# Holding TensorE to source order in the delta-rule stage of a hybrid block

## The chip, the cores and the metric

The kernel runs on one core of one Trainium2 chip. The metric is device time in microseconds (us) of one execution. Of TensorE (PE, with its weight loads PEld), VectorE (DVE), ScalarE (ACT), GpSimd (POOL) and the DMA queues (issued by SP), each runs its own instruction stream in order and meets the others at semaphores.

## The reference

One layer on a sequence of 2048 tokens with 1024 channels, all in float32:

```python
h = rms_norm(x, mix_norm_g); proj = h @ w_in          # 3*512 + 4*512 + 8 columns
y_a = short_conv_mixer(a_h, a_b, a_c, ...)             # b * conv3(c * hx), normed per group of 64
y_b = gated_deltanet(d_q, d_k, d_v, d_z, beta, alpha)  # conv4 + silu, chunked delta rule, norm, gate
x = x + concat([y_a, y_b]) @ w_out
x = x + hier_moe(rms_norm(x), ...)                     # 4 groups x 8 experts, top 2
return rms_norm(x, final_norm_g)

# gated delta rule, per chunk and head
uw = triangular_solve(eye + L, [v * beta, k_beta * exp(g)])
v_new = u_i - w_i @ state
o_i = qd_i @ state + a_i @ v_new
state = state * exp(gl_i) + kd_i.T @ v_new
```

## The kernel before

The program has three stages. The first, up to about 941 us of the profiled span, computes the input projection together with the two mixers; the second multiplies by `w_out` and routes; the third runs the experts. The change touches only the first.

The first stage is cut into 16 **units**, one for each of 4 heads and 4 blocks of 512 tokens (`units`, head outermost). A unit goes through three steps, written as Python generators that yield between pieces:

- `stage1` does four projections (q, k, v, z) with `project`. One projection is 24 matmuls of 128x128 by 128x512 in float16 (the rows `acc<-hT,whl`, L134), because both operands are split in a high and a low half, and it yields after every fourth. ACT copies each result out, DVE runs the four-tap convolutions (`cv`, L298, L301), ACT and DVE the silu (`sg`, L305 to L310).
- `stage2` takes `cv` to the matrices of the delta rule: transposes of k (`d<-id,cv`, L326), decays (`grow,sel` L342, then ACT's exponential `eG` L345 that reads the same PSUM tile, then a mask that is added to that tile, `mneg` L346, then ACT's `DT` L349), k·k and q·k products (`d<-cv`, L363), and on DVE the solve of the 16x16 diagonal blocks (`Ts`, L389 to L391).
- `stage3` completes the inverse by doubling (L420 to L461) and runs the scan over four chunks of 128 tokens: `r<-Sn,kq` (L472), DVE's `xr`, `r<-xr,U` (L477), DVE's `vn`, `r<-vn,kd` (L483), DVE's new state `Sn`, and the outputs `o` (L491, L492). It ends with ACT's square of `o` (`osq`, L497), DVE's sum (L498), a matmul with a constant matrix (`d<-osq,omean`, L501), and ACT, DVE and POOL work (L96, L97, L503, L504) up to the output `yh`.

From the fifth unit on (`FIRST = NB`, that is 4) each unit also carries one piece of the short-convolution mixer: `conv_a`, three more projections, DVE work (L545 to L552), ACT's square (`osq`, L554), a matmul `pn<-osq,bones` (L557), ACT's L96 and L97, DVE's L559, and a split into `yh` by ACT (L92) and DVE (L93). Its `osq` and the `osq` of `stage3` are the same single buffer (pool `one`, one buffer a tag).

In the source, unit `i`'s projections are written together with `stage2` of unit `i-1` and `stage3` of unit `i-2`: `merge` takes 43 steps of `main` (one step is four projection matmuls), and between them spreads 18 steps of `stage2` and 21 of `stage3`. What is left of each is run out after the 43rd step, `main` first. But the source's order doesn't bind TensorE: a planner orders every engine's instructions when the program is built, by when it reckons their inputs to be there and by priority (steps of older units have priority 1000), so that projection matmuls of a later unit can stand ahead of a step that is written earlier. PSUM holds two projection results (`accp`), three tiles `d`, two `r` and one `o`.

Of the kernel before, what the change touches and what calls it, by code (L numbers as in the profile page):

```python
# [38 lines left out]
def hybrid_block(ctx, tc, x, mix_g, w_in, ca_w, ca_g, dn_w, a_log, dt_bias, dn_g, w_out,  # L39
                 ffn_g, rg_w, re_w, w_gate, w_up, w_down, fin_g, out, dbg=None):  # L40
    nc = tc.nc
    dbg = dbg or {}
    V, A, G, T = nc.vector, nc.scalar, nc.gpsimd, nc.tensor

    consts = ctx.enter_context(tc.tile_pool(name="consts", bufs=1))
    dram = ctx.enter_context(tc.tile_pool(name="dram", bufs=1, space=DRAM))
# [32 lines left out]
    def seq(*gs):  # L79
        for g in gs:  # L80
            yield from g
# [18 lines left out]
    with ExitStack() as ph1:  # L100
# [39 lines left out]
        def slices(g, n):  # L140
            for _ in range(n):
                if next(g, 0) == 0:
                    return
                yield 1

        def merge(main, others, steps=24):

            others = [[o[0], o[1], 0, o[2] if len(o) > 2 else 1000] for o in others]
            for i in range(steps):
                if main is not None and next(main, 0) == 0:  # L150
                    main = None
                for o in others:
                    while o[0] is not None and o[2] * steps < (i + 1) * o[1]:
                        o[2] += 1
                        with tc.high_priority(o[3]):
                            if next(o[0], 0) == 0:
                                o[0] = None
            for g in [main] + [o[0] for o in others]:
                for _ in g or ():
                    pass  # L160

        dn = ph1.enter_context(ExitStack())
        if True:
# [30 lines left out]
            def prep(b, xs=None):  # L194
                ss = two.tile([P, CB], F32, name="ss")
                for c in range(CB):
                    xt = xs[c] if xs else load_x(b, c)
                    pool, tag = (whlp, "whl") if b else (lng, "kq")
                    hh = pool.tile([P, 2, D], F16, name="hh", tag=tag)
                    A.activation(hh[:, 0], xt, AF.Square, accum_out=ss[:, c:c + 1])  # L200
                    (G if b > 1 or b and c % 2 else V).tensor_tensor(xt, xt, gmix, op=OP.mult)
                    rsqrt(ss[:, c:c + 1], ss[:, c:c + 1], 1.0 / D)
                    split(hh[:, 0], hh[:, 1], xt, ss[:, c:c + 1])
                    if b and PSPL:
                        yield 1
                    for i in range(2):
                        pt = dp.tile([P, KT, P], F16, name="d")
                        for k in range(KT):
                            pin(T.transpose(pt[:, k, :], hh[:, i, k * P:(k + 1) * P], id16), b and PPIN)
                        (A.copy if b>1 and i else V.tensor_copy)(hT[b][:, i, :, c * P:(c + 1) * P], pt)  # L210
                    yield 1
# [350 lines left out]
            def load_ws(key, cols):  # L562
                ws = wcache.setdefault(key, [])
                for c0 in cols:
                    ws.append(load_w(c0))
                    yield 1

            def cols_a(m):
                return [c0 + P * m for c0 in (1024, 0, 512)]

            FIRST = NB
# [7 lines left out]
            def main(i):  # L579
                yield from main1(i)  # L580
                if i >= FIRST:
                    yield from conv(i - FIRST)
# [108 lines left out]
            for i in range(len(units) + 2):  # L691
                others = []
                if 0 <= i - 2:
                    others.append((stage3(*units[i - 2]), S3N, S3P))
                if 0 <= i - 1 < len(units):
                    others.append((stage2(*units[i - 1]), S2N, S2P))
                if i < NB:
                    others.append((gate_cols(i) if i else gt0, GTN, GTP))
                if i + 1 < NB:
                    others.append((prep(i + 1), PREP[i], PRP))  # L700
                if i < len(units) and i % NB == NB - 1:
                    h = i // NB + 1
                    new = [load_ws(h, [1536 + 512 * q + P * h for q in range(4)])] if h < H else []
                    new.append(load_ws(H + h - 1, cols_a(h - 1)))
                    others.append((seq(*new), 7 if h < H else 3))
                if i < len(units):
                    merge(main(i), others, 43 if i >= FIRST else 24)
                else:
                    merge(slices(rest, 32), others)
            dn.close()  # L710

            o1 = ctx.enter_context(tc.tile_pool(name="o1", bufs=2, side="right", reuse_waits="tile"))
# [835 lines left out]
```

## Time and profile before

| | |
|---|---|
| median of 3 runs | 1977.12 us (1973.57 to 1978.59) |
| the profiled execution | 1979.14 us, of which the span 1977.4 us |
| busy over the span | PE 1768.5 us (89%), DVE 1414.9 (72%), ACT 1016.1 (51%), POOL 492.0 (25%) |
| 203 to 941 us, fifth unit to the last of the mixers | PE busy 711.93 of 738.00 us, DVE 506.45, ACT 267.39, POOL 107.94 |

Times below are microseconds from the start of the span. A row of the timeline gives start, duration, engine, line, operation, output and inputs, shapes, count, and in square brackets how long the engine had stood idle before it and what it had waited for. A float32 matmul is two or more PE instructions.

### The profile page before, as it was taken

Reading aid. Unit: us, or ns where it says so; the run is one execution under the profiler, and the core shown is the slowest. Engines: PE = TensorE matmul, PEld = TensorE weight load, DVE = VectorE, ACT = ScalarE, POOL = GpSimd, SP = SyncE. Lnnn points to the kernel's source line nnn. Section 1 sums busy time; section 2 is a strip of 40 time slices with the busy share of each in tenths; the row PEclk is TensorE's granted clock in tenths of the full one; section 3 lists DMA queues with packets and bytes.
Section 4 is the critical chain, followed back from the end, with each engine's and each line's share of the span. In section 5 each row is a group of like instructions: output and inputs, shape, how many; then the busy total and the mean of one; then the engine's idle time right before and its main releaser. Section 6 shows DMA issues by size and latency. Waiting matters only on the chain. (4 is left out here: it accounts for less than half of the span.)

```text
span 1977.4 us, 43048 instructions
## 1 busy us (share of the span) xinstructions
PE 1768.5 (89%) x16783; PEld 1218.5 (62%) x16783; DVE 1414.9 (72%) x2756; ACT 1016.1 (51%) x1700; POOL 492.0 (25%) x408
## 2 busy tenths in 40 slices
PE   6789999999999999999899998999899999999830
PEld 5455555555555455554354466988788999999720
DVE  8899776776678666764444858887778888888623
ACT  6655333443334333322433656766677777777622
POOL 1321111111111111101000114233222443443366
PEclk9889999999999999999999999999999999999965
DMA  4221000110002000101656868999999999999854
GB/s 152 71 73 52 10 14 14 55 47 14 14 24 77 9 14 9 35 20 41 213 172 230 303 215 267 340 295 293 297 318 358 358 343 347 340 341 300 275 164 146
DMA packets 203764, 329.26 MB, mean 167 GB/s; under 512 B 45021, under 2 KB 99366, under 8 KB 203554
## 3 DMA queue, kind: packets, MB, share of 16 engines
q1 hardware_dynamic: 177010, 264.90, 39.5%
q0 software_dynamic: 22016, 52.48, 10.2%
q10 hardware_dynamic: 4528, 9.06, 1.2%
q8 instruction: 134, 2.20, 0.4%
q14 instruction: 76, 0.62, 0.1%
HBM read 276.21 MB, written 54.53 MB: 167 GB/s over the span
## 5 line engine op out<-in xcount | busy, mean ns | idle before, releaser
L134 PE MATMUL acc<-hT,whl 128*128 128x512 f16 x2640 | 637.7, 382 | 0.5 <-DVE hT L210 0.3
L1080 PE MATMUL a<-xT,wgu 128*128 128x136 f16 (+19 forms) x6528 | 401.3, 224 | 16.5 <-DVE sl L1087 15.6
L1080 PEld LDWEIGHTS <-wgu 128*128 128x128 f16 x6528 | 395.0, 99 | 22.0 <-issue 17.6
L134 PEld LDWEIGHTS <-whl 128*128 128x128 f16 x2640 | 252.9, 99 | 250.1 <-issue 12.4
L93 DVE SCALAR_TENSOR_TENSOR wgu<-mst,gw,wgu 128x1024 f16<-128x1024 f32 x256 | 317.2, 1276 | 16.6 <-ACT wgu L92 13.9
L92 ACT ACTIVATE wgu<-mst,gw 128x1024 f16<-128x1024 f32 x256 | 279.7, 1138 | 32.0 <-DMA mst<-in_w_up_dram 30.2
L1000 PE MATMUL a<-wo,yb 128*128 128x512 f16 x768 | 177.9, 381 | 5.3 <-ACT wo L92 3.8
L1093 POOL DMA_INDIRECT acc_d<-yo,tabS x53 | 101.0, 1905 | 256.0 <-ACT yo L1141 204.9
L93 DVE SCALAR_TENSOR_TENSOR wd<-mst,wd 128x1024 f16<-128x1024 f32 x128 | 154.4, 1214 | 6.5 <-ACT wd L92 6.5
L1150 PE MATMUL a<-ac,wd 128*128 128x136 f16 (+12 forms) x1920 | 143.1, 230 | 4.4 <-ACT ac L92 4.1
L92 ACT ACTIVATE wd<-mst 128x1024 f16<-128x1024 f32 x128 | 130.8, 1046 | 27.2 <-DMA mst<-in_w_down_dram 26.3
L1150 PEld LDWEIGHTS <-wd 128*128 128x128 f16 x1920 | 130.3, 98 | 7.7 <-issue 6.0
L1000 PEld LDWEIGHTS <-yb 128*128 128x128 f16 x768 | 71.8, 98 | 86.2 <-issue 11.4
L301 DVE SCALAR_TENSOR_TENSOR cv<-raw,pcol,cv 128x512 f32<-128x512 f32 x144 | 120.1, 834 | 2.2
L1049 POOL DMA_INDIRECT xr<-h_d,tabG x54 | 69.1, 1280 | 169.4 <-PE t L1065 147.3
L1087 DVE SCALAR_TENSOR_TENSOR sl<-a,sl 128x136 f32<-128x136 f32 (+19 forms) x136 | 39.5, 292 | 78.7 <-ACT sl L1086 78.3
L1086 ACT ACTIVATE sl<-a 128x136 f32<-128x136 f32 (+19 forms) x136 | 37.1, 275 | 100.8 <-PE a L1080 98.0
L1115 PE MATMUL pl<-wd,ac 128*120 128x512 f16 (+6 forms) x336 | 80.4, 384 | 0.7 <-ACT ac L92 0.7
L1054 POOL DMA_INDIRECT gs<-gt_d,gix x54 | 76.4, 1415 | 16.3 <-issue 15.4
L1137 PE MATMUL pl<-id,yt 128*128 128x128 f32 (+13 forms) x320 | 55.3, 293 | 27.9 <-ACT yo L1141 18.5
L389 DVE TENSOR_TENSOR pr<-Ts,fs 32x1 f32<-32x1 f32 (+14 forms) x240 | 74.7, 311 | 5.2 <-DMA fs<-dscr 1.4
L92 ACT ACTIVATE ac<-sl 128x136 f16<-128x136 f32 (+19 forms) x136 | 41.9, 310 | 63.7 <-DVE sl L1087 63.6
(359 smaller groups left out, 2578.7 us busy)
## 6 DMA issues: line engine op xcount, KB each, us to landing
mst<-in_w_gate_dram SPq DMA_DIRECT2D x256, 256.0 KB
mst<-in_w_up_dram SPq DMA_DIRECT2D x256, 256.0 KB
mst<-in_w_down_dram SPq DMA_DIRECT2D x128, 512.0 KB
wst<-in_w_in_dram SPq DMA_DIRECT2D x28, 512.0 KB
xt<-in_x_dram SPq DMA_DIRECT2D x16, 512.0 KB
ydr<-yh SPq DMA_DIRECT2D x64, 128.0 KB
yb<-ydr SPq DMA_DIRECT2D x16, 512.0 KB
x<-in_x_dram SPq DMA_DIRECT2D x16, 512.0 KB
```

The costliest lines, as they stand in the source:

```text
L92: A.activation(hi, src, AF.Copy, scale=scale)
L93: (eng or V).scalar_tensor_tensor(lo, src, scale, hi, op0=OP.mult, op1=OP.subtract)
L134: T.matmul(acc, w[:, i, k, :], hT[b][:, j, k, :], start=(n == 0), stop=(n == 3 * KT - 1))
L301: V.scalar_tensor_tensor(y, tap(j), pcol[:, q:q + 1], y, op0=OP.mult, op1=OP.add)
L389: V.tensor_tensor(q, Ts[:, 0:i, 0:i].rearrange("p j m -> p m j"), bc(fs[:, None, 0:i, i], [32, i, i]), op=OP.mult)
L1000: T.matmul(po, yb[:, i, k, c * P:(c + 1) * P], wo[:, j, k, n * FF:(n + 1) * FF], start=(q == 0), stop=(q == 3 * KT - 1))
L1049: G.indirect_dma_start(out=xr[0:cw].rearrange("p a k c -> p (a k c)"), out_offset=None, in_=h2_d[0:end, :], in_offset=IO(ap=ix, axis=0))
L1054: G.indirect_dma_start(out=g[0:cw], out_offset=None, in_=gt_d[0:end * NE, :], in_offset=IO(ap=gx, axis=0))
L1080: T.matmul(pg[:, q, 0:n], wq[:, i, k, q, f * P:(f + 1) * P], xT[:, j, k, 0:n], start=(z == 0), stop=(z == 3 * KT - 1))
L1093: st = G.indirect_dma_start(out=acc_d, out_offset=IO(ap=sx, axis=0), in_=yo[0:cw], in_offset=None, bounds_check=S - 1, oob_is_err=False, c ...
L1115: T.matmul(py[0:n], ac[:, i, k, 0:n], wd[:, j, k, q * FF:(q + 1) * FF], start=(z == 0), stop=(z == 3 * FF // P - 1))
L1150: T.matmul(pg[:, u, 0:n], wd[:, i, k, d * P:(d + 1) * P], ac[:, j, k, 0:n], start=(z == 0), stop=(z == 3 * FF // P - 1))
```

## The change

All TensorE instructions now go through a small wrapper. While `pinned[0]` is set, each instruction is tied behind the TensorE instruction that was written before it. It is set from the unit with index 4 to the end of the loop over units (two more rounds, which hold only older units' steps and the remaining mixer pieces), and cleared behind it. No operation, tile or size changes, and nothing is tied on the other engines.

```diff
-    V, A, G, T = nc.vector, nc.scalar, nc.gpsimd, nc.tensor
+    V, A, G = nc.vector, nc.scalar, nc.gpsimd
+    pinned = [False]
+
+    class InOrder:
+        def __getattr__(self, name):
+            f = getattr(nc.tensor, name)
+
+            def call(*args, **kw):
+                ins = f(*args, **kw)
+                return tc.keep_in_program_order(ins) if pinned[0] else ins
+
+            return call
+
+    T = InOrder()
...
+                pinned[0] = i >= FIRST
                 if i < len(units):
                     merge(main(i), others, 43 if i >= FIRST else 24)
                 else:
                     merge(slices(rest, 32), others)
+            pinned[0] = False
             dn.close()
```

In the built program the number of TensorE instructions is the same (16,136 matmuls). Their order differs from the 1,185th to the 4,473rd; ACT, DVE, POOL and SP are reordered in the same stage alone. Every TensorE instruction now bears the wrapper's line, L53, and lines of other engines stand 15 higher.

**The seam between two units, on TensorE.** Before, where the unit with index 4 ends and the next begins (`acc_2736` is the last projection of the one, `acc_2804` the first of the other; `pn` is the mixer's norm, `r`, `o` and `d<-osq` belong to the scan of an older unit):

```order
L134 MATMUL acc_2736<-hT0_90,whl_2276 128x512
L483 MATMUL r_2782<-vn_2759,kd_1961 128x128
L491 MATMUL o_2599<-kq_1959,Sn_2725 128x128
L492 MATMUL o_2599<-it_1968,vn_2759 128x128
...
L134 MATMUL acc_2804<-hT1_91,whl_1937 128x512
L472 MATMUL r_3060<-Sn_2784,kq_2391 128x128
L557 MATMUL pn_2772<-osq_2770,bones_495 128x512
...
L134 MATMUL acc_2882<-hT1_91,whl_1997 128x512
L501 MATMUL d_2791<-osq_2788,omean_472 128x512
```

The same seam in the changed program:

```order
L53 MATMUL acc_2736<-hT0_90,whl_2276 128x512
L53 MATMUL pn_2772<-osq_2770,bones_495 128x512
L53 MATMUL r_2782<-vn_2759,kd_1961 128x128
L53 MATMUL o_2599<-kq_1959,Sn_2725 128x128
L53 MATMUL o_2599<-it_1968,vn_2759 128x128
L53 MATMUL d_2791<-osq_2788,omean_472 128x512
L53 LDWEIGHTS whl_1937
L53 MATMUL acc_2804<-hT1_91,whl_1937 128x512
```

Before, 3 and then 22 projection matmuls of the next unit stood around `pn` and ahead of `d<-osq,omean`; now no projection matmul stands between the last of one unit and `omean`, and the next unit's first four come behind it.

**Behind the seam, on ScalarE.** Before, from the scan's L96 on (`junk` and `kn` are norms of k, `yh` is the older unit's output, `eG` what the mask matmul `mneg` waits for):

```order
L96 ACTIVATE osq<-d,eps_69 128x512
L330 ACTIVATE junk,kn<-d 128x128
L345 ACTIVATE eG<-d 128x512
...
L331 ACTIVATE kn<-kn,eps 128x4
...
L349 ACTIVATE DT<-d,kn 128x128 x4
L92 ACTIVATE yh<-osq 128x512
```

And in the changed program (L111 is the old L96, L345 the old L330, L107 the old L92, L360 the old L345):

```order
L111 ACTIVATE osq<-d,eps_69 128x512
L112 ACTIVATE osq<-osq 128x512
L345 ACTIVATE junk,kn<-d 128x128 x3
L107 ACTIVATE yh<-osq 128x512
L345 ACTIVATE junk,kn<-d 128x128
L346 ACTIVATE kn<-kn,eps 128x4
L360 ACTIVATE eG<-d 128x512
```

The split of `yh`, which needs POOL's product L504, has moved from behind `DT` to ahead of `eG`. On TensorE the four `grow,sel` matmuls and `mneg` now stand next to each other, with one step of four projection matmuls, `d<-id,cv` and two more such steps between `omean` and them; before, a projection matmul and two `d<-cv` lay between `grow,sel` and `mneg`.

**Where the ordered part begins, on TensorE.** Before, the last chunk of the scan that is written beside the fourth unit:

```order
L491 MATMUL o<-kq,Sn 128x128
...
L134 MATMUL acc<-hT_90,whl 128x512
L477 MATMUL r<-xr,U 128x128
...
L134 MATMUL acc<-hT_90,whl 128x512
L483 MATMUL r<-vn,kd 128x128
L492 MATMUL o<-it,vn 128x128
...
L134 MATMUL acc<-hT_90,whl 128x512
L501 MATMUL d<-osq,omean 128x512
```

Now the whole of that scan, of which this is the end, stands without them:

```order
L53 MATMUL r<-Sn,kq 128x128
L53 MATMUL o<-kq,Sn 128x128
L53 MATMUL r<-xr,U 128x128
L53 MATMUL r<-vn,kd 128x128
L53 MATMUL o<-it,vn 128x128
L53 MATMUL d<-osq,omean 128x512
L53 LDWEIGHTS whl
L53 MATMUL acc<-hT_90,whl 128x512
```

63 projection matmuls of the fifth unit (`hT_90` is its block) that stood between the steps from `d<-Tm,E` (64x64) to `omean` have moved behind them.

## Rows read from the trace of the kernel before

**Rows 1.** Windows, from one omean to another: length, busy PE, PEld, DVE, ACT, POOL, clock.

```profile
304.42:358.15 53.73, 52.76 (x301) 27.65 (x302) 35.75 (x85) 19.30 (x40) 7.59 (x8) 1.00 0.05 13
...
248.49:850.23 601.74, 582.14 (x3294) 311.60 (x3294) 423.90 (x945) 224.61 (x446) 89.72 (x86) 0.98 0.10 27
```

**Rows 2.** PE's waits from 203 to 945 us: total, times, longest.

```profile
PE o L491 <- DVE kn L335: 11.9, 6, 2.0
PE d L363 <- ACT DT L349: 3.8, 7, 1.4
PE d L501 <- DVE osq L498: 3.7, 12, 0.3
PE pn L557 <- ACT osq L554: 3.3, 1, 3.3
PE r L472 <- DVE Sn L488: 1.6, 3, 0.9
```

**Rows 3.** Timeline of PE around the seam that ends the unit with index 4.

```profile
240.69 0.38 PE L483 MATMUL r<-vn,kd 128*128 128x128 f32 x2
...
241.36 0.81 PE L134 MATMUL acc<-hT,whl 128*128 128x512 f16 x3
...
242.30 1.13 PE L557 MATMUL pn<-osq,bones 128*128 128x512 f32 x2
243.27 4.91 PE L134 MATMUL acc<-hT,whl 128*128 128x512 f16 x22
248.49 1.10 PE L501 MATMUL d<-osq,omean 128*128 128x512 f32 x2 [0.31 <-DVE osq L498]
249.42 0.60 PE L326 MATMUL d<-id,cv 128*128 128x128 f32 x4
249.95 0.39 PE L342 MATMUL d<-grow,sel 48*128 48x128 bf16 x4
...
255.28 0.46 PE L491 MATMUL o<-kq,Sn 128*128 128x128 f32 x2 [2.02 <-DVE kn L335]
```

**Rows 4.** Timeline of DVE at the same seam.

```profile
240.90 0.69 DVE L552 SCALAR_TENSOR_TENSOR ucv<-acc,ucv 128x512 f32<-128x512 f32 x1 [0.30 <-PE acc L134]
...
244.85 0.75 DVE L559 SCALAR_TENSOR_TENSOR osq<-ucv,pcol,osq 128x512 f32<-128x512 f32 x1 [2.07 <-ACT osq L97]
...
247.65 0.69 DVE L498 TENSOR_TENSOR osq<-osq,q 128x512 f32<-128x512 f32 x1 [0.66 <-ACT osq L497]
...
254.39 0.74 DVE L503 SCALAR_TENSOR_TENSOR osq<-o,pcol,osq 128x512 f32<-128x512 f32 x1
```

**Rows 5.** Timeline of ACT at the same seam.

```profile
243.47 0.69 ACT L96 ACTIVATE osq<-pn,eps 128x512 f32<-128x512 f32 x1 [1.22 <-PE pn L557]
...
247.02 0.60 ACT L497 ACTIVATE osq<-o 128x512 f32<-128x512 f32 x1 [0.76 <-DVE yh L93]
...
249.62 0.69 ACT L96 ACTIVATE osq<-d,eps 128x512 f32<-128x512 f32 x1
...
250.46 0.60 ACT L345 ACTIVATE eG<-d 128x512 f32<-128x512 f32 x1
...
256.51 0.63 ACT L92 ACTIVATE yh<-osq 128x512 f16<-128x512 f32 x1
```

**Rows 6.** Timeline of POOL behind the same seam.

```profile
255.21 1.27 POOL L504 TENSOR_TENSOR osq<-osq,zr 128x512 f32<-128x512 f32 x1 [1.28 <-DVE kn L334]
```

**Rows 7.** Window of DVE's load where the ordered part will begin, columns as in rows 1.

```profile
180.00:200.00 20.00, 19.59 (x117) 11.17 (x115) 18.39 (x59) 9.53 (x12) 1.74 (x2) 1.00 0.10 28
```

**Rows 8.** Windows of PE's waits and what followed them; clock is third from the end.

```profile
256.00:260.00 4.00, 4.00 (x17) 3.25 (x16) 3.49 (x9) 1.06 (x3) 0.48 (x1) 0.57 0.19 65
...
474.50:482.00 7.50, 7.50 (x30) 5.72 (x29) 4.28 (x11) 0.74 (x2) 0.15 (x1) 0.54 0.16 42
...
585.05:592.00 6.95, 6.95 (x42) 4.64 (x42) 5.98 (x14) 3.31 (x7) 1.20 (x1) 1.00 0.14 41
...
937.39:940.73 3.34, 0.00 (x0) 0.00 (x0) 2.52 (x4) 0.63 (x1) 0.97 (x10) 1.00 1.06 316
```

## The prediction

> **What bounds the kernel now.** I first read the windows from one `omean` to the next, which is one unit. The steady unit without a long wait takes 53.73 us, of which PE is busy 52.76, and the mean over eleven units is 601.74 / 11 = 54.70 us [rows 1]. DVE, the next, is busy 35.75. So this stage is bound by PE, and it is as long as PE's work plus PE's own gaps. Then I read PE's waits from 203 to 945 us [rows 2]: 12 of the scan's `omean` wait 0.31 us each, six `o` matmuls wait about 2 us each, and little else. All waits of the stage before the tail's `pn` sum to 11.9 + 3.8 + 3.7 + 1.6 = 21.0 us. The reader should see that a wait at the head of PE's stream stops all that stands behind it: at 253.26 PE stood idle 2.02 us in front of an `o` matmul [rows 3], although ready projection matmuls came next.
>
> What matters most is the seam [rows 3]. Its first non-projection instruction starts at 240.69, when the last projection of the unit is done, and `omean` starts at 248.49. Between lies a chain through other engines: DVE's L552, ACT's square, `pn` (starts 242.30), ACT, DVE's L559, the split of `yh` by ACT and DVE (L93), only then ACT's square of the scan's output (L497 at 247.02), because both squares use the one buffer `osq`, then DVE's L498 and `omean` [rows 3 to 5]. Each link starts when the one before it ends. `omean` waited only 0.31 us because 3 + 22 projection matmuls filled these 7.80 us.
>
> **The change part by part.** PE's instructions stay the same, so only gaps and the clock move. I sum gaps.
>
> *The seam chain, new.* Now no projection matmul lies in those 7.80 us. PE has `pn` (242.30 to 243.27 = 0.97 us) and up to three scan matmuls (0.67 us, 240.69 to 241.36, where three fillers began) [rows 3]. Idle: 7.80 - 0.97 - 0.67 = 6.16 us. In the changed order six of the 12 seams have all three scan matmuls there, three have two (about 6.4 us idle), three have none (6.8 us): 6 x 6.16 + 3 x 6.4 + 3 x 6.8 = 76.6 us. The chain can't start earlier, since its first link needs the last projection, and it has no slack that a free DVE or ACT would remove: L552 to L498 follow each other at the distance of the operations themselves [rows 4, 5]. The one place where `pn` already stood bare, at the stage's end, waited 3.3 us [rows 2], more than the 1.6 us (240.69 to 242.30) that I count here.
>
> *Behind the seam, new.* `mneg` now follows `grow,sel` directly and needs ACT's `eG`, which stands behind the split of `yh`, and so behind POOL's L504. From `omean`'s start: ACT's L96 at +1.13 (248.49 to 249.62) [rows 3, 5]; L503 1.38 us after it, as L559 follows the other L96 (243.47 to 244.85) [rows 4, 5]; POOL 0.82 after L503 begins (254.39 to 255.21) [rows 4, 6]; `yh` 1.30 after that (256.51) [rows 5]; then `yh` itself 0.63 and `eG` 0.60 [rows 5], and two small ACT steps between them, which have no row here (my estimate is 0.35 each, about half of one with 512 columns): +6.6 us. PE itself is there after `omean` 0.93, `d<-id,cv` 0.53 [rows 3], twelve projection matmuls at 216 ns (4.91 us for 22, less the pipelined end, 4.75 / 22) 2.6, and `grow,sel` 0.39: +4.4 us. It waits 2.2 us, at 13 seams 28 us. Lower bound 0.7 (an ACT that is free: from the end of `grow,sel`, 250.34, to the end of `eG`, 251.06 [rows 3, 5]), that is 9 us. I take the upper one, because ACT runs its stream in order.
>
> *Where the ordered part begins.* 63 projection matmuls, 63 x 0.216 = 13.6 us, lose their place between the steps of a scan. The scan shrinks only as far as DVE allows: DVE is busy 18.39 of 20.00 us there [rows 7], so some 2.5 us at most return. Cost 11 us, bounds 6 and 13.6.
>
> *Inside a unit.* Scan steps now stand eight projection matmuls (1.73 us) apart, in one place four. DVE's streams of small solve steps (L389, L391) and taps run between. I expect one wait of half a us in most units, 6 us; bounds 0 and 24 (twelve units at 2 us, the longest scan wait shown is 0.9 [rows 2], twice).
>
> *The tail.* Two rounds with fewer projections have an `omean` and an inversion step without cover: 5 us, bounds 2 and 9. After it, the 3.3 us of `pn` [rows 2], in which DVE was splitting later weights, may shrink: -3 us, bounds 0 and -6.
>
> *Removed.* The 21.0 us of waits above. `o` is now written beside `kd`, late in the scan, when L503 has long freed its buffer, so the 11.9 us don't come back elsewhere.
>
> *The clock.* After the wait at 253.26 the granted clock was 0.57 over 4.00 us, that is its lower level, 1.2 GHz, for 3.4 us; after another 0.54 over 7.50 us (from 474.50); after the one that ended at 585.05 it was 1.00, and 1.00 too through the 3.34 us idle at 937.39 [rows 8]. Of the six long waits five lost the clock, 4 x 3.4 + 6.9 = 20.5 us at half, which costs 10 us, now saved. At the 13 seams I charge one such episode each, half of 3.4 us: 22 us; bounds 0 (as after 937.39) and 44 (twice as long, as from 474.50).
>
> The Trainium skill (TensorE: Matmul & The Clock Gate, HAM oscillation) describes a kernel whose array fell back to half rate at every tile because a wait recurred at each. By that rule all 13 seams pay and the charge stands; the trace shows it at five of six such waits and not at the longest, so without it the sum would be 22 us lower.
>
> *Sum.* 76.6 + 28 + 11 + 6 + 5 - 3 - 21 - 10 + 22 = +114.6 us. On the profiled execution's 1979.14 us that gives 2093.7; the median of the runs shown lies 2.0 lower, so 2092 us. What follows the stage keeps its order on every engine, and so moves with it.
>
> **The rivals.**
> 1. *The seam costs, but less.* If `eG` comes early (9 for 28), no clock is lost (0 for 22) and the scan has no waits (0 for 6): 2092 - 47 = 2045 us. For it speaks the clock of 1.00 at 937.39 [rows 8]; against it ACT's order.
> 2. *The clock stays low around the seams.* Three gaps of 1.6, 4.5 and 2.2 us within some 14 us may hold the half clock twice as long: +22, 2114 us. For it speaks the episode of 6.9 us, against it the full clock after two of the waits [rows 8].
> 3. *The scan becomes the bound.* PE can no longer run on while DVE is late, and DVE's queue puts solve steps, taps and the silu product between scan operations. If each of four chunks waits 0.9 us [rows 2], 12 x 4 x 0.9 = 43 us instead of 6: 2129 us. Against it: DVE is busy two thirds of a unit only [rows 1].
> 4. *Faster: the seam is covered.* If the next unit's first matmuls, which are ready, kept PE fed, the seam's wait would be what `omean` shows now, 0.31 us [rows 2]. Then 12 x 0.31 + 11 - 21 - 10 = -16 us, 1977 - 16 = 1961 us. This decides from a seam below about 1.7 us: 12 x 1.7 = 20, what is saved net. Against it speak both rows of the order: they stand behind `omean`, and PE did not pass the blocked `o` either [rows 3].
>
> That the change does nothing is ruled out by the built order.
>
> **How the numbers follow.** The forecast of 2092 us gets 0.60, rival 1 0.12, rival 2 0.13, rival 3 0.12, rival 4 0.03. The likeliest is the forecast. The range runs from rival 1, 2045, to a little past rival 3, 2135. About 0.3% (6 us) is what a measurement can tell from no change; rivals 1 to 3 and the forecast all lie far above it. Faster 0.03, same 0.01, slower 0.96.
>
> **What would show each step.** In the profile after: waits of PE in front of `pn` of about 1.6 us and in front of `omean` of about 4.5 us, twelve of each; of `mneg` on `eG` of about 2 us; no wait of `o` on L503 or L335; units of 62 to 64 us instead of 54.7; PE's clock below 1 behind the seams. I am wrong if `omean` waits much less than 4 us (then its chain had slack), if units lengthen by waits of `r` matmuls on DVE (rival 3), or if the stage keeps its length.

## The result, and the profile after

| | before | after |
|---|---|---|
| time, median of the runs | 1975.77 us (1973.57 to 1978.59) | 2082.75 us (2081.24 to 2086.97) |
| ratio | | 1.0544, 95% interval 1.0522 to 1.0566 |
| profiled execution: time, span | 1979.14, 1977.4 us | 2082.03, 2080.2 us |
| mean granted clock of TensorE | 0.962 | 0.939 |

The change costs 107 us. The forecast was 2092 us (2045 to 2135), slower. The head of the page after:

```profile
span 2080.2 us, 43041 instructions
...
PE 1793.2 (86%) x16783; PEld 1241.1 (60%) x16783; DVE 1419.7 (68%) x2756; ACT 1020.4 (49%) x1700; POOL 474.4 (23%) x408
```

The time lies where the order changed. Of the tail's last `pn`, whose start ends the stage (940.73 us before), the start is now 1046.36, or 105.6 us later; the span grew by 102.8, so what follows the stage was 2.8 us shorter. PE's waits from 180 to 1045 us (total, times, longest) show the rest, and answer to [rows 2]:

```profile
PE d L53 <- DVE osq L513: 58.9, 14, 5.1
PE pn L53 <- ACT osq L569: 19.3, 13, 1.7
PE d L53 <- ACT eG L360: 9.5, 13, 1.0
PE r L53 <- DVE Sn L503: 5.7, 10, 1.1
PE r L53 <- DVE vn L494: 4.3, 11, 0.8
PE d L53 <- DVE Tm L446: 2.5, 5, 1.4
```

All waits of this answer sum to 105.6 us (that this is also the shift of the stage is chance); the same answer for before, up to 940 us, sums to 21.4, so they grew by 84.2. The first two lines are three quarters of the sum; all but 4.5 us of them (1.41 where the ordered part begins, 3.06 in the tail) are the twelve seams. No wait of an `o` matmul is left. The other 21 us by which the stage grew are longer busy time of PE, and the windows show a lower clock. The first answers to [rows 1]: a unit from `omean` to `omean`, 61.31 us long, where the steady one took 53.73. The next three each enclose one stretch at half clock, of 6.83, 6.82 and 10.24 us: the clock, third from the end, is 0.66 over 10 us in the first, and at the lower level half is missing, so 2 x 0.34 x 10 = 6.8.

```profile
263.40:324.71 61.31, 53.54 (x299) 29.56 (x300) 37.43 (x84) 19.46 (x40) 6.11 (x8) 0.95 0.04 12
...
260.00:270.00 10.00, 6.60 (x22) 3.10 (x23) 2.71 (x5) 5.07 (x14) 1.45 (x2) 0.66 0.08 27
322.00:331.00 9.00, 6.29 (x18) 2.87 (x18) 2.13 (x3) 4.55 (x13) 1.34 (x2) 0.62 0.08 29
625.00:639.00 14.00, 8.26 (x26) 3.43 (x25) 3.80 (x7) 7.53 (x21) 1.65 (x3) 0.63 0.10 36
```

Windows of half a microsecond over the whole stage give 15 such stretches with 116.0 us at half clock, where before had 5 with 20.5. They are one of 20.5 us where the ordered part begins, one at each of the twelve seams, one in the tail, and one that starts with the tail's last `pn`.

The same seam as in [rows 3], now on PE (timeline, idle time and its releaser in brackets):

```profile
253.82 1.89 PE L53 MATMUL acc<-hT,whl 128*128 128x512 f16 x8
257.15 1.12 PE L53 MATMUL pn<-osq,bones 128*128 128x512 f32 x2 [1.44 <-ACT osq L569]
258.12 0.38 PE L53 MATMUL r<-vn,kd 128*128 128x128 f32 x2
...
263.40 2.05 PE L53 MATMUL d<-osq,omean 128*128 128x512 f32 x2 [4.45 <-DVE osq L513]
265.24 1.91 PE L53 MATMUL acc<-hT,whl 128*128 128x512 f16 x4
266.94 1.06 PE L53 MATMUL d<-id,cv 128*128 128x128 f32 x4
...
269.67 0.39 PE L53 MATMUL d<-grow,sel 48*128 48x128 bf16 x4
270.96 0.38 PE L53 MATMUL d<-mneg,idb 128*128 128x512 bf16 x1 [0.89 <-ACT eG L360]
```

From `pn` to `omean` it is 6.25 us, as before (6.19): the chain is what it was, and its cover is gone. `omean` takes 2.05 us instead of 1.10, and `d<-id,cv` 1.06 instead of 0.60: that is the half clock. ACT at the same seam, as in [rows 5]:

```profile
258.32 0.69 ACT L111 ACTIVATE osq<-pn,eps 128x512 f32<-128x512 f32 x1 [1.22 <-PE pn L53]
...
261.93 0.60 ACT L512 ACTIVATE osq<-o 128x512 f32<-128x512 f32 x1 [0.82 <-DVE yh L108]
...
269.21 0.63 ACT L107 ACTIVATE yh<-osq 128x512 f16<-128x512 f32 x1
...
270.33 0.58 ACT L360 ACTIVATE eG<-d 128x512 f32<-128x512 f32 x1
```

The square of the scan's output, L512, waits for the mixer's `yh` (L108), although the scan's last `o` matmul ended at 258.95: the two have one buffer `osq`.

### The profile page after: what moved, and what is told of

Same layout as the page of the kernel before. It is cut to its first block, busy times and chain, and to the rows that moved or that the text cites. A ratio compares the mean times of both kernels' runs of the same rounds, so it can differ in the third digit from the quotient of the medians.

```text
span 2080.2 us, 43041 instructions
## 1 busy us (share of the span) xinstructions
PE 1793.2 (86%) x16783; PEld 1241.1 (60%) x16783; DVE 1419.7 (68%) x2756; ACT 1020.4 (49%) x1700; POOL 474.4 (23%) x408
## 5 line engine op out<-in xcount | busy, mean ns | idle before, releaser
L53 PE MATMUL acc<-hT,whl 128*128 128x512 f16 (+1 forms) x2832 | 666.2, 378 | 3.8 <-DVE hT L225 3.1
L53 PEld LDWEIGHTS <-whl 128*128 128x128 f16 x2832 | 270.1, 101 | 280.7 <-issue 50.4
L53 PE MATMUL a<-xT,wgu 128*128 128x136 f16 (+19 forms) x6528 | 401.2, 224 | 16.9 <-DVE sl L1104 16.0
L53 PEld LDWEIGHTS <-wgu 128*128 128x128 f16 x6528 | 394.9, 99 | 22.5 <-issue 18.1
L108 DVE SCALAR_TENSOR_TENSOR wgu<-mst,gw,wgu 128x1024 f16<-128x1024 f32 x256 | 317.1, 1275 | 15.3 <-ACT wgu L107 15.1
L107 ACT ACTIVATE wgu<-mst,gw 128x1024 f16<-128x1024 f32 x256 | 279.5, 1138 | 32.8 <-DMA mst<-in_w_up_dram 28.6
L53 PE MATMUL a<-wo,yb 128*128 128x512 f16 x768 | 179.0, 382 | 4.1 <-ACT wo L107 3.5
L108 DVE SCALAR_TENSOR_TENSOR wd<-mst,wd 128x1024 f16<-128x1024 f32 x128 | 154.4, 1215 | 5.2 <-ACT wd L107 5.1
L53 PE MATMUL a<-ac,wd 128*128 128x136 f16 (+12 forms) x1920 | 142.7, 230 | 1.9 <-ACT ac L107 1.7
L107 ACT ACTIVATE wd<-mst 128x1024 f16<-128x1024 f32 x128 | 130.7, 1046 | 20.7 <-DMA mst<-in_w_down_dram 19.9
L53 PEld LDWEIGHTS <-wd 128*128 128x128 f16 x1920 | 130.2, 98 | 4.9 <-issue 3.2
L53 PEld LDWEIGHTS <-yb 128*128 128x128 f16 x768 | 72.2, 98 | 86.3 <-issue 12.1
L316 DVE SCALAR_TENSOR_TENSOR cv<-raw,pcol,cv 128x512 f32<-128x512 f32 x144 | 109.0, 757 | 0.5
L569 ACT ACTIVATE osq<-ucv 128x512 f32<-128x512 f32 x15 | 9.4, 627 | 158.8 <-DVE ucv L567 158.8
L53 PE MATMUL pl<-wd,ac 128*120 128x512 f16 (+6 forms) x336 | 81.4, 388 | 1.0 <-ACT ac L107 1.0
L53 PE MATMUL d<-osq,omean 128*128 128x512 f32 x32 | 29.8, 1032 | 58.9 <-DVE osq L513 58.9
L1071 POOL DMA_INDIRECT gs<-gt_d,gix x54 | 75.6, 1401 | 16.4 <-issue 15.4
L53 PE MATMUL pl<-id,yt 128*128 128x128 f32 (+13 forms) x320 | 55.4, 292 | 27.6 <-ACT yo L1158 18.3
```

The source lines that it names most:

```text
L53: ins = f(*args, **kw)
L107: A.activation(hi, src, AF.Copy, scale=scale)
L108: (eng or V).scalar_tensor_tensor(lo, src, scale, hi, op0=OP.mult, op1=OP.subtract)
L316: V.scalar_tensor_tensor(y, tap(j), pcol[:, q:q + 1], y, op0=OP.mult, op1=OP.add)
L569: A.activation(osq, cv, AF.Square)
L1071: G.indirect_dma_start(out=g[0:cw], out_offset=None, in_=gt_d[0:end * NE, :], in_offset=IO(ap=gx, axis=0))
```

## Experiments

Kernels own_buffer, warm_seams, carry_tails and one_unit ran beside a before of 1977.4 us; pin_o, own_before, own_split and carry_all beside one of 1983.6, late_start and own_before_split beside one of 1982.3. In these two groups what follows the stage is longer in every kernel (from the tail's last `pn` to the end of the span 1045.3 us in pin_o and 1045.0 in own_before, against 1036.7 in before's profile). So kernels of different groups are compared by their ratio to before, or by places in the stage. The expectations were reckoned from a before of about 1977 us.

**own_buffer: the changed kernel, the two chains apart.**

```diff
-                osq = one.tile([P, TB], F32, name="osq")
+                osq = one.tile([P, TB], F32, name="osq2")
```

> The changed kernel, but the scan's osq gets a buffer of its own, so that its square of o needn't wait for the mixer's split of yh. Theory (the seam's chain is bare, and the shared buffer makes it long): pn to omean falls from 6.2 us to some 3.3 us (ACT's Ln, square, DVE's sum), omean's waits from 58.9 to about 25 us in total, time 2040 to 2055 us. Rival (the chain is set by the engines' order, not by the buffer): waits and time as in the changed kernel, about 2083 us. Rival (the clock, not the waits, costs the time): waits fall, time stays above 2070 us.

Measured: 2022.3 us, ratio 1.0226 (1.0194 to 1.0258), 60 us less than the changed kernel and 18 below the range expected, which counted the waits (58.9 us expected to fall to 25, now 21.4) and not the clock that came back with them. TensorE's order is the same, instruction by instruction. The seam on PE, and the waits (the 22.6 of `pn` hold the last one's 3.3, ahead of which the list of the changed kernel ends):

```profile
255.93 1.13 PE L53 MATMUL pn<-osq,bones 128*128 128x512 f32 x2 [1.45 <-ACT osq L569]
...
259.98 1.10 PE L53 MATMUL d<-osq,omean 128*128 128x512 f32 x2 [2.25 <-DVE osq L513]
...
265.97 0.38 PE L53 MATMUL d<-mneg,idb 128*128 128x512 bf16 x1 [1.55 <-ACT eG L360]
```

```profile
PE pn L53 <- ACT osq L569: 22.6, 14, 3.3
PE d L53 <- DVE osq L513: 21.4, 11, 2.3
PE d L53 <- ACT eG L360: 16.9, 13, 1.5
```

`omean` comes 4.05 us behind `pn` instead of 6.25. So it is at six of the twelve seams; at three, where two of the scan's matmuls stand behind the last projection, it is 3.21 us, and at the three where none does, 0.96. PE's gaps at the seam no longer cost the clock: 23.9 us at half in 2 stretches are left, one where the ordered part begins and one that starts just behind the tail's last `pn`. Since the order is the same, the window over the same eleven units weighs the clock by itself (columns as in [rows 1]; first the changed kernel, then own_buffer):

```profile
263.40:938.50 675.10, 592.12 (x3293) 325.27 (x3294) 425.25 (x945) 228.06 (x446) 73.14 (x86) 0.94 0.09 24
```

```profile
259.98:879.00 619.02, 563.98 (x3293) 314.78 (x3294) 419.83 (x946) 226.08 (x446) 75.31 (x86) 1.00 0.10 26
```

The same 3293 matmuls are busy 592.1 us with and 564.0 without the stretches at half clock: 28.1 us, 2.6 per seam. The other 28 us of the difference are gaps. And the wait on `eG` nearly doubled, from 9.5 to 16.9 us: at half clock PE itself comes later to `mneg`, so part of what the clock costs had been paid out of that wait.

Between different orders, PE's busy time can't be read as clock alone. Three windows from the `omean` ahead of the ordered part to the tail's last `pn` hold the same work (before, the changed kernel, own_buffer):

```profile
161.10:940.73 779.63, 751.21 (x4361) 404.99 (x4360) 545.27 (x1244) 286.37 (x582) 115.22 (x134) 0.99 0.10 28
```

```profile
162.26:1046.36 884.10, 772.38 (x4362) 427.75 (x4361) 548.62 (x1244) 290.79 (x582) 96.47 (x134) 0.94 0.09 25
```

```profile
161.04:982.64 821.60, 739.79 (x4362) 415.80 (x4361) 543.14 (x1244) 288.68 (x582) 98.92 (x134) 0.99 0.10 27
```

Before and own_buffer both have 20.5 us at half clock in them, and own_buffer is busy 11.4 us less. A part can be that its half clock falls beside waits, the rest that the order or the modelled ends of matmuls change what counts as busy; no run settles it. So the 21.2 us by which the changed kernel is busier than before are a balance: 32.6 us more than own_buffer, which has the same order without the lost clock of the seams and the tail, and 11.4 less for the rest.

**warm_seams: work without a reader in the seam's gaps.** 6 matmuls of 128x512 ahead of `pn` and 18 ahead of `omean`, whose product nobody reads; nothing is left out.

```diff
+                warm(18)
                 pn = dp.tile([P, TB], F32, name="d")
...
+            def warm(n):
+                if pinned[0]:
+                    pd = rp.tile([P, TB], F32, name="r")
+                    for k in range(n):
+                        T.matmul(pd, id16, hT[0][:, 0, 0, :], start=True, stop=True)
...
+                warm(6)
                 pn = at("pn", [P, TB])
```

> The changed kernel with matmuls that nobody reads added in the gaps: 6 of 128x512 in front of each pn, 18 in front of each omean. They should end about when the wait would have ended. Theory (waits and clock both cost; the half clock about a quarter of the loss): half clock falls from 116 us to under 40 us, time 2050 to 2065 us. Rival (the half clock lies under the waits and costs nothing): time 2080 to 2095 us, since the added matmuls can only delay.

Measured: 2070.6 us, ratio 1.0476 (1.0438 to 1.0514). The clock is full at every seam (23.9 us at half in 2 stretches), yet only 12 us came back, and the time is 6 us above the range expected. PE's waits in it:

```profile
PE d L53 <- ACT eG L360: 18.6, 13, 1.5
PE d L53 <- DVE osq L513: 10.2, 13, 1.4
```

The wait on `eG` is 18.6 us, near own_buffer's 16.9 and 9.1 more than in the changed kernel. Over the same eleven units the window is 917.75 - 261.21 = 656.5 us long, 18.6 less than 675.1, and 28.1 (the clock) - 9.1 (the wait) gives 19.0. So a third of what the clock cost had been taken out of the next wait. In the tail the added matmuls cost 4.5 us (from the last seam's `omean` to the last `pn` 112.4 against 107.9), which is why the whole gained less.

**own_split: own_buffer with a step more between `grow` and `mneg`.**

```diff
                 A.activation(eG, pG, AF.Exp)
+                yield 1
...
-            S2N = 18
+            S2N = 19
```

> The changed kernel with the buffer of own_buffer, and with one step more between the four matmuls of grow and the one of mneg, so that eight projection matmuls stand between them. It asks what the wait of mneg on ACT's eG is worth by itself at a full clock (16.9 us in 13 waits in own_buffer, 9.5 in the changed kernel). Theory A: the wait is a cost of its own, and it goes whole: 2022.3 - 16.9 = 2005 us, 2002 to 2010, and no wait on eG above 0.5 us. Rival: ACT is late for what follows as well, and the second half of the wait turns up in d<-cv, which waits for DT: 2014 to 2024 us.

Measured: 2021.6 us, ratio 1.0196 (1.0175 to 1.0216), against 1.0226 for own_buffer. The wait on `eG` is gone; what stayed:

```profile
PE pn L53 <- ACT osq L570: 22.6, 14, 3.4
PE d L53 <- DVE osq L514: 21.4, 11, 2.3
PE r L53 <- DVE vn L495: 6.6, 12, 1.6
```

From the fifth unit's `omean` to the tail's last `pn` it takes 973.21 - 264.75 = 708.5 us, in own_buffer 982.64 - 259.98 = 722.7: of the 16.9 us, 14.2 came. The wait was a cost of its own there, as theory A said, and it didn't turn up at `DT`, which is waited for once (1.9 us). But theory A's time was missed: the whole lies where the rival had it, and it gained only 0.3% (the two intervals overlap). The first `omean` of the ordered part starts 4.4 us later than in own_buffer (205.8 against 201.4), with 27.3 us at half clock around it instead of 20.5; how the step more brings that about, no run shows.

**carry_tails: the seam's steps spread into the next unit.** The norm of the mixer's unit and the last steps of the scan are handed over and issued among the first dozen steps of the next unit.

```diff
...
+            if keep is not None:
+                return tail(main or iter(()), keep[0])
...
-                    merge(main(i), others, 43 if i >= FIRST else 24)
+                    left = merge(main(i), others, 43 if i >= FIRST else 24, [s3] if i >= FIRST else None)
```

> The changed kernel, order still bound, but what a unit leaves undone after its 43 steps (the mixer's norm, the scan's last steps) is written between the first dozen steps of the next unit instead of in one piece at the seam. Theory (bare seams cost nearly all): waits in front of pn and omean fall from 78 to under 8 us, the half clock from 116 to under 50 us, time 1980 to 1992 us (the 13 us of the place where the ordered part begins stay). Rival (the bound order itself, through scan steps that wait for DVE, costs it): time above 2040 us.

Measured: 2000.7 us, ratio 1.0112 (1.0083 to 1.0142): 82 us of the 107 are gone, though TensorE still keeps the order of the source. So it is the place of these steps that costs, and not the fixed order as such. It missed the range expected by 9 us; its two longest waits show where:

```profile
PE d L53 <- DVE osq L533: 14.0, 5, 3.7
PE d L53 <- ACT eG L380: 11.9, 13, 0.9
```

**carry_all: carry_tails with both edits of own_split.**

> carry_tails with both edits of own_split: the seam's steps spread into the next unit, a buffer of its own for the scan's osq, and a step between grow and mneg. It asks whether the order of the source can cost nothing once each chain has projection matmuls beside it. Theory A: what carry_tails still lost is 14.0 us before omean and 11.9 before mneg, both of which go, while the 13 us at the stage's beginning stay: 2000.7 - 14 - 11.9 + 4 for small waits inside a unit = 1979 us, 1974 to 1986, so that it ends within 0.5% of before. Rival: the waits go from these two to the steps behind them (d<-cv on DT, the scan's r on xr and vn), because the chain through ACT and DVE in the first dozen steps is what is full: 1992 to 2002 us.

Measured: 1997.4 us, ratio 1.0075 (1.0055 to 1.0096), 7 us less by the ratio (the intervals overlap), where theory A wanted 22. The rival holds: the two waits are 3.0 us and nothing now, and others took their place:

```profile
PE d L53 <- ACT DT L385: 12.2, 11, 1.5
PE r L53 <- DVE xr L510: 6.7, 5, 2.4
```

**one_unit: the order kept for the fifth unit alone.**

```diff
-                pinned[0] = i >= FIRST
+                pinned[0] = i == FIRST
```

> The changed kernel, but the order is bound for the unit with index 4 alone, so that the seam behind it is filled by unbound projections of the next unit. Theory (the place where the order begins loses 63 matmuls of cover, some 13 us, each later seam 6 to 8 us): time 1985 to 1992 us. Rival (PE catches up, the beginning is free, all lies in the seams): 1974 to 1978 us.

Measured: 1990.7 us, ratio 1.0062 (1.0040 to 1.0084), inside the range expected. This is the price of the beginning and the inside of one unit: `omean` at the end of the fifth unit starts 15.0 us later than before (263.53 against 248.49, behind the same 721 projection matmuls), and the tail's last `pn` 11.6 (952.33 against 940.73). In the changed kernel the beginning looks so on PE:

```profile
185.68 0.56 PE L53 MATMUL r<-xr,U 128*128 128x128 f32 x2 [1.57 <-ACT U L477]
...
197.32 0.80 PE L53 MATMUL r<-Sn,kq 128*128 128x128 f32 x2 [1.15 <-DVE Sn L503]
...
202.37 2.07 PE L53 MATMUL d<-osq,omean 128*128 128x512 f32 x2 [1.41 <-DVE osq L513]
```

The scan's float32 steps stand alone, wait for DVE and ACT, and run at half clock (20.5 us at half from 186 on): 0.80 us for a pair that takes 0.44 in before's seam (at 242.01).

**late_start: the order kept from the sixth unit on.**

```diff
-                pinned[0] = i >= FIRST
+                pinned[0] = i > FIRST
```

> The changed kernel, with the order of the source kept from the sixth unit on instead of from the fifth. It asks what the term of the ordered part's beginning is made of. Theory A: the cost there is that of catching up, in whatever unit the order begins, with the projection matmuls that the free scheduler had put ahead, and it moves with the beginning. Then the time falls only by what the fifth unit itself cost, one seam with its wait on eG and its steps inside: 2083 - 7 = 2076 us, 2071 to 2080. Rival: the cost belongs to that one place, where the scan's float32 steps stand alone on TensorE at half clock because the units before it have no mixer projections, and beginning a unit later leaves it out: 2083 - 7 - 13 = 2063 us, 2056 to 2068.

Measured: 2077.7 us, ratio 1.0476 (1.0435 to 1.0517), that is 13 us less than the changed kernel by the ratio; the tail's last `pn` is 15.4 us earlier (1030.94). That lies between the two sums. Both had taken off a seam that is still there: since the sixth unit's projections can't pass the fifth's last steps, all twelve seams are bare here too, and all twelve lose the clock. Of the waits before `omean`, only the one where the changed kernel begins is gone (14 there, 58.9 us):

```profile
PE d L53 <- DVE osq L513: 58.1, 13, 5.1
```

What is saved lies ahead of the first seam's `omean`, which starts at 247.29 instead of 263.40, behind the same 696 projection matmuls: 16.1 us, the beginning and the inside of the fifth unit. From there to the tail's last `pn` it takes 783.7 us, in the changed kernel 783.0, so no such cost has moved along to the new beginning. Theory A is out (its range is met only because the before of this group is slower), and the rival holds in substance: the cost belongs to that one place. That agrees with the 15.0 us of one_unit. The window of half clock from 186 on is gone.

**pin_o: before, one instruction held in order.**

```diff
-                        T.matmul(pO[:, c], St, kq[:, c, 1], start=True, stop=False)
+                        pin(T.matmul(pO[:, c], St, kq[:, c, 1], start=True, stop=False), True)
```

> The kernel before, in which one instruction alone is held to the order of the source: the matmul o<-kq,Sn now stands right behind r<-vn,kd of its chunk instead of where the scheduler put it, ahead of the second half of the keys' product. It asks what the waits of the row o [rows 2] were worth, the term of 21 us that the prediction gave back. Theory A: those waits (11.9 us in 6) and the half clock that they start (2 of the 5 stretches of before, 7 us at half) go, and nothing is late behind them: 12 to 22 us less, 1955 to 1965 us, and no wait on o of over 1 us in the trace. Rival: the same ACT work is then waited for one step later, by the second half of d<-cv on DT, so that the time stays at 1970 to 1978 us and waits of about 2 us stand on the line of DT.

Measured: 1987.9 us, ratio 1.0016 (0.9998 to 1.0034). The rival holds: nothing is gained (its range was for the faster before). PE's waits:

```profile
PE d L363 <- ACT DT L349: 17.7, 13, 2.1
```

The waits on `o` were 11.9 us in 6 and those on `DT` 3.8 in 7 [rows 2]: together 15.7, now 17.7 in one place. What was late in before is ACT's work behind the seam, and whichever matmul comes next pays for it.

**own_before: before, with the buffer of own_buffer.**

> The kernel before, with a buffer of its own for the scan's osq, the edit of own_buffer. It asks whether the shared buffer costs anything as long as the order is free. Theory A: in the kernel before TensorE has 22 projection matmuls between pn and omean, so the 2.2 us by which the buffer of its own shortens the chain (6.25 to 4.05 us in the two kernels that keep the order of the source) lie beside work: 1974 to 1980 us, within 0.3% of before, and omean's waits stay at 3 to 5 us in sum. Rival: the chain also delays what ACT and DVE do behind it, the gates that o waits for: 1962 to 1970 us.

Measured: 1966.0 us, ratio 0.9912 (0.9893 to 0.9932). The rival's time holds; by the ratio the gain is larger than it said, and this is faster than both kernels. Its reason doesn't hold: the gates that `o` and `DT` wait for are waited for as long as before, 10.9 + 5.0 = 15.9 us against 15.7 [rows 2], only in shorter pieces.

```profile
PE o L491 <- DVE kn L335: 10.9, 9, 1.2
```

A later seam on PE, first in before, then here:

```profile
298.23 1.12 PE L557 MATMUL pn<-osq,bones 128*128 128x512 f32 x2
299.19 4.91 PE L134 MATMUL acc<-hT,whl 128*128 128x512 f16 x22
304.42 1.10 PE L501 MATMUL d<-osq,omean 128*128 128x512 f32 x2 [0.31 <-DVE osq L498]
```

```profile
297.15 1.13 PE L557 MATMUL pn<-osq,bones 128*128 128x512 f32 x2
298.11 1.02 PE L501 MATMUL d<-osq,omean 128*128 128x512 f32 x2
```

With a buffer each, the two chains run side by side, the scheduler puts `omean` right behind `pn` (in ten seams; three projection matmuls lie between in the other two), and the 22 projection matmuls that it had spent as cover for the seam stand elsewhere. From the first `omean` shown to the tail's last `pn` the same 4065 matmuls take 721.1 us instead of 738.8 (busy and length, first before, then own_before):

```profile
201.92:940.73 738.81, 712.74 (x4065) 382.10 (x4064) 507.50 (x1139) 268.00 (x538) 108.60 (x129) 0.99 0.10 27
```

```profile
201.76:922.87 721.11, 700.30 (x4065) 376.18 (x4065) 495.85 (x1139) 262.78 (x538) 106.88 (x129) 1.00 0.10 28
```

5 us of the 17.7 are idle time of PE, 3.7 of them `omean`'s own waits [rows 2]. 12 are busy time, of which half clock explains about half of 20.5 - 4.5 = 16.0, so 8: of before's five stretches none is left, one of 3.4 us stands at 212, and one more begins 1.1 us ahead of the window's end. The rest, some 4 us, can be that the ends of matmuls are modelled and the groups are cut differently; it isn't settled.

**own_before_split: own_before with a step more between `grow` and `mneg`**, the edit of own_split.

> The kernel before, with a buffer of its own for the scan's osq and a step more between grow and mneg: both edits of own_split, with the order left free. It asks whether what is still waited for in own_before (o 10.9 us in 9, d<-cv on DT 5.0 in 4, both on ACT's work of the seam) can be had by moving mneg away from grow. Theory A: eG comes no later and DT only by the step, there are more matmuls beside both, and half of the 16 us goes: 1955 to 1962 us where own_before gave 1966. Rival: as in pin_o, what is late is ACT and not one step, so the wait changes its place alone: 1963 to 1970 us.

Measured: 1972.1 us, ratio 0.9935 (0.9912 to 0.9958); its interval overlaps that of own_before, and it is no better. That is the rival's outcome, though not its reason. The waits on `o` fell from 10.9 to 7.3 us and those on `DT` from 5.0 to 2.5, but the part from the first `omean` on takes 927.69 - 206.14 = 721.6 us, as in own_before (721.1), and that `omean` comes 4.4 us later, as it did in own_split.

## Why the prediction was right, step by step

The mechanism and its places were as predicted, and the sum, +114.6 us, was close to the span's +102.8. That it was so close is partly luck: two terms were wrong in opposite directions.

- **The seam chain**, 76.6 us: right. The twelve seams show 17.8 us before `pn` (1.44 to 1.67 each; 1.6 forecast) and 55.9 before `omean` (4.45 to 5.06; 4.5 forecast), 73.7 in all. One link of the chain was named and not weighed: the one buffer `osq`. own_buffer shows 2.2 us of six seams, 3.0 of three and 5.2 of three to be that buffer. To say that the chain had no slack was true of free engines, not of buffers.
- **Behind the seam**, 28 us (bounds 9 and 28): mis-sized; 9.5. At full clock both sides can be read in own_buffer: `grow` ends 4.44 us behind the start of `omean` (4.4 forecast) and `mneg` starts at 5.99, where the forecast's ACT would have been done at 6.6; so 1.3 us each (16.9 in 13) instead of 2.2, because ACT was put 0.6 too late. The larger error is that both were timed at full clock, while the text charged that same seam with a lost one. In the changed kernel `grow` ends 6.7 us behind `omean` and `mneg` starts at 7.6: half clock delays PE by 2.2 us and `eG` by 1.6, and 0.7 us of wait is left at most seams.
- **The clock**, +22 - 10 us: mis-sized downwards. All twelve seams lost it, ten for 6.8 us and two for 10.2, not for 3.4. At 2.6 us a seam (own_buffer's window) that is 31 us. Less the 10 saved that is 21, as much as the stage grew beyond its waits, but this agreement is chance: the sum leaves out the 20.5 us at half clock where the ordered part begins and the 3.4 in the tail, and at equal half clock the ordered program is busy less than before (own_buffer, 11.4 us). The prediction kept rival 2 as another outcome; what it describes, several gaps that hold the clock low for twice as long, did occur, and the waits' term took most of it back. The Trainium skill (TensorE: Matmul & The Clock Gate, HAM oscillation) describes a kernel that fell back to half rate at every tile, and by it the prediction charged every seam. The changed kernel agrees, twelve of twelve; in own_buffer waits recur at each seam too, shorter ones, and the clock stays.
- **The clock and the wait on `eG` are one term, not two.** Together 28 + 22 = 50 us were forecast; together they measure about 9.5 + 31 = 41. warm_seams shows the exchange.
- **Where the ordered part begins**, 11 us (6 to 13.6): 13.3. The stretch from `d<-Tm,E` (64x64) to `omean` kept its length, 20.59 against 20.89 us, with 63 matmuls (13.6 us) fewer in it. The scan gained only 0.3 us of the 2.5 allowed; that it ran at half clock is the likely reason, and no run isolates it. one_unit (15.0) and late_start (16.1) show this price together with the inside of the fifth unit, and late_start that it belongs to this place.
- **Inside a unit**, 6 us: 7.8 (waits on `Sn`, `vn`, `xr` and `Tm` behind the beginning and up to the last seam). Rival 3 is out.
- **The tail**, 5 us: 7.3 (an `omean` 1.56, a `pn` 1.50, an inversion step 1.36 and 0.63 on `Tm`, 0.64 on `Sn`, and 1.65 on `DT`). **After the stage**, -3 us: -2.8, but this is luck. The last `pn` waits 3.35 us, as before, so it isn't where the 2.8 come from; and in the four kernels that ran beside the before of 1977.4 us this part is 1037.5 to 1041.5 us long, longer than in before's profile (1036.7), not shorter (1033.8 in the changed kernel's).
- **Removed**, 21.0 us: right for this change, since no `o` wait is left, but the reason was half true. pin_o puts the `o` matmul where the changed kernel has it and the wait comes back on `DT`. In the changed kernel a wait on `DT` is left only once (1.65 us, counted in the tail). That PE stands still at the seam, so that ACT has time there, is the likely reason; no run isolates it.
- **Rival 4** (the seam covered) is out: PE didn't pass its blocked `omean` in any of the twelve seams.

With the sizes that the runs show, the terms of the stage sum to 73.7 + 9.5 + 13.3 + 7.8 + 7.3 - 21 - 10 + 31 = 111.6 us, 6 more than its 105.6. The busy time that the order itself changes, named above, is the likely difference; it isn't settled.

## What to carry to other kernels

An order in program sequence is as good as the place that the source gives to steps which hang on a chain through other engines: spread over the next unit (carry_tails), the same rigid order costs 1.1% instead of 5.4%. Where two chains follow each other link by link, look for a shared buffer before anything else; here a second one gave 60 us in the ordered kernel and 0.9% even in the one whose scheduler had hidden the chain behind 22 projection matmuls. And time a wait behind a gap at the clock that the gap leaves: a lost clock and the next wait pay for each other, and a wait that is removed at one instruction is gained only if the engine behind it is not late for the next one too.

## What the runs showed of the hardware

The length of a gap alone didn't tell whether the clock would fall. In before, a gap of 2.02 us in front of an `o` was followed by 3.4 us at half clock [rows 3, 8]; after five of six such waits (1.94 to 2.02 us) it fell, after the one that ended at 585.05 it didn't. In own_buffer gaps of 1.45, 2.25 and 1.55 us within 12 us left it at 1.00; the window begins behind the first of them:

```profile
255.93:266.50 10.57, 6.77 (x33) 3.67 (x34) 4.36 (x8) 7.46 (x22) 2.28 (x3) 1.00 0.11 38
```

With 1.44 to 1.67 and 4.45 to 5.06 us in the changed kernel it was lost at every seam, for 6.8 or 10.2 us, two or three times as long as in four of before's five stretches. And where the ordered part begins, 20.5 us at half in the changed kernel and 27.3 in own_split went with waits of which none exceeded 1.6 us: there PE had the scan's small float32 matmuls alone, with short waits between them (ten of 0.34 to 1.57 us from 183 to 202 us in the changed kernel).
